# Two token-major value projections of a decoder layer as seven half-size products each, with the retention's tail among the first head products

## The chip, the core and the metric

The kernel runs on one core of a Trainium2 chip. A core has TensorE (PE; its weight loads are listed apart as PEld), VectorE (DVE), ScalarE (ACT), GpSimd (POOL) and SyncE (SP), which here only issues DMAs. The metric is the device time of one execution in microseconds (us), the median of the runs.

## The reference, cut to what matters

One layer of a hybrid decoder over 1024 prompt tokens and 8 decode tokens (one row for each of 8 samples), all float32. The part that the change touches is the mixer's input projection and what uses its value columns:

```python
hp = rmsnorm(xp, norm_mix[l])
qa, ka, va, qr, kr, vr, gr = project(hp, w_in[l])      # one product, columns split
oa = diff_attention_prompt(qa, ka, va, rel_bias, lam)  # 4 heads
s_p, o_r = retention_prompt(rotary(qr, pos_p), rotary(kr, pos_p) * kr_scale, vr.astype(f32), lg)
xp = xp + merge_groups(oa, o_r, gr, subln_a[l], lam_init).astype(xp.dtype) @ w_out[l]
...
v_prompt = jnp.stack(vp_l)                             # va is an output as well
```

`va` and `vr` are each (1024 tokens x 1024 inputs) times (1024 x 512); `gr` (the gate) and `[qr, kr]` have the same size. The retention goes through 8 chunks of 128 tokens with a state; its output is normed per head and multiplied by silu of the gate. After the mixer come memory attention and a squared-ReLU MLP.

## The kernel before, in words

**Operands.** Every large product is made from two float32r halves of each operand, a high part and what is left: high x high, high x low, low x high, three instructions that add up in one PSUM bank (`mm3`, and `mm`, line 67, through which nearly all products are issued). The inputs transposed, with the norm's gain in, lie in `UH` and `UL` (8 depth tiles of 128, 1032 columns: 1024 tokens and 8 decode rows). The norm's per-token factor `rstd1` is put on the results. Weights come in units of 128 x 1024 from `in_wall`: `unit` (line 103) issues the read on SP into a ring of three `raw` buffers, casts the high part on ACT (line 109, `wh`) and subtracts on DVE (line 110, `wl`); the rings of `wh` and `wl` have four slots.

**Order before.** (1) Query and key of the retention (`qkps`, 8 token tiles, 192 products of 512 columns) while the inputs arrive; the decode rows follow as 16 products with 40 and 8 weight columns (`decproj`, line 260). Then the token-major inputs are read again for the sums of squares (line 217), and GpSimd makes `rstd1` (line 121). (2) Retention values `vr`: 8 tiles x 24 products, with the decode rows put in between for the first two tiles (`tokproj`, `tokproj_parts`, `scaled`); the rotations of query and key run on DVE and GpSimd beside them (lines 336 to 338). (3) Three small products make the rows of the relative bias, which go through DRAM (`brow`, `brep`). (4) The retention, chunk by chunk, with the products of the gate (`grp`, 24 of 512 columns) cut into segments of 3, 4 and 1 depth tiles (`SEG`) between the small products of a chunk: transposes `tr`, scores `sc`, state `st`, output `op`. The norm and gate of a chunk (`head_norm_gate`, lines 380 to 384) run on ACT, GpSimd and DVE during the next chunk, and then `to_operand` transposes it (`trR`), splits it and stores it in DRAM (lines 393 to 396). `decode_step` does the decode rows' state. (5) Attention values `va`: 8 tiles x 24 products and decode rows; each tile is scaled on ACT and written to the output `v_p`. (6) The attention heads: `head_proj(h)` gives key and query of a head in 6 results of 24 products of 344 columns (line 67, tile `qkp`, with `UH` as the moving operand), `load_part` splits them, `fetch_values` reads `v_p` back (line 685) and `load_values` splits it (lines 695 and 697), `scores`, `turn`, `weigh` do the attention; `head_proj` of later heads is the filler between those products.

**What sets the order.** A planner orders the instructions of each engine by the order in which they are written and by when it expects operands; buffers of a tag go round, and a tile waits until the users of the slot's last tile are done. `pin[0] = True` keeps TensorE's products in the order written, and `tc.issue_after(ins)` puts the instructions of its block behind `ins` on the same engine. Each engine, and each DMA queue (SP's for most reads, ACT's, POOL's), takes its instructions in order.

## Time and profile before

| what | us |
|---|---|
| median of 3 runs | 1522.92 |
| lowest and highest run | 1519.58 and 1525.88 |
| span of the profiled execution | 1520.2 |
| TensorE busy in it | 1493.8 |
| VectorE, ScalarE, GpSimd busy | 1064.7, 653.3, 420.0 |

The span goes from the first instruction to the last; the runs' times hold some us around it. A row of the chain of waits gives start, length, engine, tile, line and the number of instructions. A row of a group gives line, engine, operation, out<-in, shapes and count, then the busy time in us and the mean of one in ns, then the idle time of the engine before these instructions and what ended it. `128*128 128x512` on a product is the weights' size and the moving operand's. Rows of the windows view give the stretch, its length, the busy time of PE, PEld, DVE, ACT and POOL with the number of instructions, the granted clock, the DMA share and GB/s. "SPq" is SP's DMA queue.

### The profile page before, as it was taken

The numbers are of one execution on the slowest core, as the hardware profiler recorded it, in microseconds if no ns is written. First come the engines' busy times: TensorE is split into PE (matmuls) and PEld (weight loads), VectorE is DVE, ScalarE is ACT, GpSimd is POOL, SyncE is SP. The second block draws the span as 40 slices with busy tenths as digits, with TensorE's granted clock in tenths as the row PEclk, the third lists the DMA queues.
The fourth block names the chain that finished last, engine by engine and source line by source line (L and its number), as shares of the span: only waits on it lengthen the run. The fifth ranks groups of instructions, "written<-read, shape, count | busy, mean of one in ns | idle before, by whom it ended". The sixth has DMA issues, their size and how long they took to land.

```text
span 1520.2 us, 26998 instructions
## 1 busy us (share of the span) xinstructions
PE 1493.8 (98%) x10587; PEld 1397.2 (92%) x10587; DVE 1064.7 (70%) x2112; ACT 653.3 (43%) x1276; POOL 420.0 (28%) x442
## 2 busy tenths in 40 slices
PE   9999999999999999999999999999999999999998
PEld 8778878999759999989999999999999999999997
DVE  4334503988865835567796978888889879787885
ACT  6423322665642432047535633333334434333454
POOL 0352212114412521124122224443335202020360
PEclk9999999999999999999999999999999999999998
DMA  8554424314755257453392334444435784636213
GB/s 299 174 147 128 103 90 110 84 51 126 232 172 218 79 206 189 128 186 104 125 338 78 117 131 148 154 140 152 142 140 164 266 281 116 191 84 195 86 43 113
DMA packets 121107, 229.25 MB, mean 151 GB/s; under 512 B 14209, under 2 KB 73712, under 8 KB 120852
## 3 DMA queue, kind: packets, MB, share of 16 engines
q1 hardware_dynamic: 89860, 172.13, 35.8%
q0 software_dynamic: 20160, 37.95, 8.2%
q10 hardware_dynamic: 10960, 17.45, 3.1%
q8 instruction: 83, 1.36, 0.4%
q14 instruction: 44, 0.36, 0.1%
HBM read 168.14 MB, written 57.52 MB: 148 GB/s over the span
## 4 chain that ended last, share of the span: by engine, by line
PE 81%; DVE 9%; DMA 4%; ACT 2%; issue 2%; POOL 0%; SPq 0%; DVEq 0%; ACTq 0%
PE dn L2000 18%; PE Z L1835 8%; PE qkp L67 7%; PE mq L67 6%; PE pr_o L67 6%; PE Y L1835 5%; PE X L1835 4%; PE pr_m L67 4%; PE vap L67 3%; PE vrp L67 3%; PE grp L67 3%; PE sp L67 2%; PE av L67 2%; PE mpv L67 1%; DVE wu L1650 1%
## 5 line engine op out<-in xcount | busy, mean ns | idle before, releaser
L2000 PE MATMUL dn<-UH,wd 128*128 128x258 f32 x1792 | 325.1, 283 | 1.6 <-ACT wd L1978 0.9
L2000 PEld LDWEIGHTS dn<-UH,wd 128*128 128x128 f32 x1792 | 277.8, 189 | 2.5 <-DVE c L2104 1.1
L2000 PE MATMUL dn<-UL,wd 128*128 128x258 f32 x896 | 253.0, 282 | 0.0
L2000 PEld LDWEIGHTS dn<-UL,wd 128*128 128x128 f32 x896 | 169.2, 189 | 0.0
L1861 ACT ACTIVATE hq<-r 128x258 f32<-128x258 f32 x128 | 53.7, 420 | 159.8 <-DVE r L1860 159.8
L2104 DVE TENSOR_TENSOR c<-c,dn 128x258 f32<-128x258 f32 x216 | 88.3, 417 | 32.5 <-PE dn L2000 31.0
L1835 PE MATMUL Z<-T_h,wu 128*128 128x258 f32 x512 | 100.0, 287 | 1.7 <-DVE u L1894 1.5
L1650 DVE TENSOR_TENSOR wu<-raw_up,wu 128x512 fp32r<-128x512 f32 x96 | 92.5, 965 | 9.5 <-ACT wu L1649 9.4
L1835 PE MATMUL X<-UH,wu 128*128 128x258 f32 x512 | 97.5, 282 | 0.0
L110 DVE TENSOR_TENSOR wl_u<-raw_u,wh_u 128x1024 fp32r<-128x1024 f32 x46 | 58.6, 1279 | 51.2 <-ACT wh_u L109 50.9
L1978 ACT CAST wd<-raw_d 128x512 fp32r<-128x512 f32 x96 | 58.5, 618 | 76.7 <-PE dn L2000 72.1
L109 ACT CAST wh_u<-raw_u 128x1024 fp32r<-128x1024 f32 x50 | 52.2, 1048 | 77.3 <-PE mq L67 42.9
L1835 PEld LDWEIGHTS Z<-T_h,wu 128*128 128x128 f32 x512 | 81.5, 189 | 4.1 <-DVE u L1894 1.9
L1971 ACT CAST UH<-raw_h 128x1032 fp32r<-128x1032 f32 x56 | 58.7, 1055 | 59.2 <-PE dn L2000 27.7
L1972 DVE TENSOR_TENSOR UL<-raw_h,UH 128x1032 fp32r<-128x1032 f32 x56 | 76.8, 1371 | 9.4 <-ACT UH L1971 9.4
L1979 DVE TENSOR_TENSOR wd<-raw_d,wd 128x512 fp32r<-128x512 f32 x96 | 75.2, 789 | 11.3 <-ACT wd L1978 11.3
L1835 PEld LDWEIGHTS X<-UH,wu 128*128 128x128 f32 x512 | 81.4, 189 | 0.2 <-ACT p L1886 0.2
L1868 POOL TENSOR_TENSOR ht<-hq 128x258 f32<-128x258 f32 x31 | 20.7, 668 | 193.2 <-ACT hq L1861 193.0
L1835 PE MATMUL Z<-T_l,wu 128*128 128x258 f32 x256 | 72.5, 283 | 0.0
L1992 POOL TENSOR_TENSOR raw_d<-raw_d,raw_d 128x512 f32<-128x512 f32 x16 | 22.0, 1378 | 182.0 <-DVE raw_d L1988 171.7
L1835 PE MATMUL X<-UL,wu 128*128 128x258 f32 x256 | 72.3, 282 | 0.0
L1649 ACT CAST wu<-raw_up 128x512 fp32r<-128x512 f32 x96 | 57.0, 610 | 27.2 <-DVE raw_up L1656 24.5
(491 smaller groups left out, 4605.6 us busy)
## 6 DMA issues: line engine op xcount, KB each, us to landing
raw_u<-in_wall SPq DMA_DIRECT2D x59, 512.0 KB, 4.5
HT<-ht POOLq DMA_DIRECT2D x32, 516.0 KB, 3.0
raw_h<-HT SPq DMA_DIRECT2D x32, 516.0 KB, 4.2
raw_up<-in_wall SPq DMA_DIRECT2D x32, 512.0 KB, 4.8
raw_d<-in_wall SPq DMA_DIRECT2D x32, 512.0 KB, 3.6
HQ<-hq ACTq DMA_DIRECT2D x32, 387.0 KB, 3.8
raw_h<-HQ SPq DMA_DIRECT2D x24, 516.0 KB, 5.2
cmk<-in_cmk SPq DMA_DIRECT2D x16, 512.0 KB, 4.7
```

The lines of the kernel that those rows point to most:

```text
L67: pinned(nc.tensor.matmul(out, l, r, start=start, stop=stop))
L110: (lo_engine or nc.vector).tensor_sub(wl[:, :n], raw[:, :n], wh[:, :n].bitcast(F32))
L1649: nc.scalar.copy(w[:, :512], src)
L1650: nc.vector.tensor_sub(w[:, 512:], src, w[:, :512].bitcast(F32))
L1835: pinned(nc.tensor.matmul(ps, l, r[:, k, :], start=first and k == 0 and x == 0, stop=k == 3 and x == 2, skip_group_check=True))
L1861: nc.scalar.activation(h[:, PLACE[quad], :], r, AF.Square)
L1971: nc.scalar.copy(h, rv)
L1972: nc.vector.tensor_sub(l, rv, h.bitcast(F32))
L1978: nc.scalar.copy(w[:, :512], src)
L1979: nc.vector.tensor_sub(w[:, 512:], src, w[:, :512].bitcast(F32))
L2000: pinned(nc.tensor.matmul(ps, l, r[:, k, cq], start=first and k == 0 and x == 0, stop=k == 3 and x == 2, skip_group_check=True))
L2104: nc.vector.tensor_add(y, y, ps)
```

## The change

The stages are put in the order 1, 5, 2, 4, 6: both value projections now stand ahead of the retention, and each is done by `token_block` as seven products q of half size (512 tokens, 512 inputs, 256 outputs; 4 token tiles x 4 depth tiles x 3 terms, two token tiles to a PSUM bank) in the order 1, 2, 6, 7, 4, 5, 3.

- **Combined inputs.** For each pair of depth tiles k and k + 4, `combine` (ACT, DVE, GpSimd) makes from the raw input rows the three combinations that the products 5, 7 and 4 need (`XT`, split in high and low), and a fourth, `t2f`, which later replaces the second half of the tokens in `UH` and `UL`, depth tiles 0 to 3, for product 6. After the products the retention's first chunks restore them from inputs that are read again (`fetch_again`, `restore`). The raw rows are kept until combined, so depth rows 3 and 7, the last to come, take the buffers of rows 0 and 4. The depth order is `KT_PAIRS` = 0, 4, 1, 5, 2, 6, 3, 7, and the weight units of query/key and of the gate are laid out to match.
- **Query and key.** Seven token tiles are done while inputs arrive, then the decode rows (`dproj`, in the eighth bank), then tile 7 alone (`last`), which takes the bank of tile 0 after `take_qk(0)`.
- **Combined weights.** `token_operands` reads the four quarters of a weight; DVE makes their sums (`s3` and others), and each product's operand is split by ACT and DVE one product ahead. The quarter 12 is read twice.
- **Results.** ACT copies product 1 and scales product 2; DVE adds the others, two banks of 512 columns each, to what is kept in SBUF. Scaling by `rstd1` is on ACT, for tiles 4 to 7 of `vr` within the retention. Decode rows go through products 1, 2, 4 and 5 with 8 instructions of 256 columns each.
- **Moved.** Rotations of tiles 8, 0, 1, 2 go into the first block and 3 to 7 into the second; the bias rows go after products 2, 6 and 7 of the first block, `brep` to chunk 3; the gate's first two units are loaded in the second block's product 5, the other two read after product 3 and split in chunk 0; ACT's silu table is loaded by a small instruction in the second block; `decode_step` is cut into pieces over chunks 0 to 3, its store goes to POOL's queue, as does the read of `rb`; the decode outputs (`opd`) go to chunk 5.
- **The tail.** The first head's units are loaded in chunk 7. After the retention come 36 products of the first head, then `to_operand` of chunk 7, then the rest.

The diff, cut to its core:

```diff
+    def behind(*engines):
+
+        st = ExitStack()
+        for e in engines:
+            last = next(x for x in reversed(nc.cur_bb.bb.instructions) if str(x.engine).split(".")[-1] == e)
+            st.enter_context(tc.issue_after(last))
+        return st
...
+    def combine(k, y1, y2):
+
+        g1, g2 = g_mix[:, k : k + 1], g_mix[:, k + 4 : k + 5]
+        t2 = t2f[k // 2][:, k % 2, :]
+        nc.scalar.activation(y1[:, f_lo], y1[:, f_lo], AF.Copy, scale=g1)
+        nc.scalar.activation(dd[:, k, :], y1[:, NT:], AF.Copy, scale=g1)
+        nc.scalar.activation(y2[:, f_lo], y2[:, f_lo], AF.Copy, scale=g2)
+        nc.vector.scalar_tensor_tensor(y1[:, f_hi], y1[:, f_hi], g1, y1[:, f_lo], ALU.mult, ALU.subtract)
+        nc.vector.scalar_tensor_tensor(t2, y2[:, f_hi], g2, y1[:, f_hi], ALU.mult, ALU.subtract)
+        nc.vector.scalar_tensor_tensor(dd[:, k, :], y2[:, NT:], g2, dd[:, k, :], ALU.mult, ALU.subtract)
+        nc.gpsimd.tensor_sub(y1[:, f_lo], t2, y1[:, f_lo])
+        nc.gpsimd.tensor_sub(y2[:, f_lo], y2[:, f_lo], t2)
+        for q, src in ((5, y1[:, f_hi]), (7, y1[:, f_lo]), (4, y2[:, f_lo])):
+            h, l = (x[:, k, :] for x in XT[q])
+            nc.scalar.copy(h, src)
+            nc.vector.tensor_sub(l, src, h.bitcast(F32))
...
+            if kt > 5:
+                combine(kt - 6, rows.pop(kt - 6), rows.pop(kt - 2))
...
+        dproj(qkps[7], units_qk)
...
+        with behind("Activation", "DVE", "Pool"):
+            combine(2, rows.pop(2), rows.pop(6))
+            combine(3, rows.pop(3), rows.pop(7))
...
+            def operand(q):
+                if q == 1:
+                    load(11)
+                    load(12, True)
+                    load(22)
+                    load(21)
+                    return split(raws[11], q)
+                if q == 2:
+                    return split(raws[12], q)
+                if q == 6:
+                    a22, a21, a11 = raws[22], raws[21], raws[11]
+                    s3 = raws[7] = G.tile([P, 1024], F32R, tag="wl", name=f"s3_{nm}", bufs=RING).bitcast(F32)
+                    nc.vector.tensor_sub(s3, a11, a21)
+                    nc.vector.tensor_sub(a11, a22, s3)
+                    return split(a11, q)
+                if q == 4:
+                    w = split(raws[22], q)
+                    nc.vector.tensor_add(raws[21], raws[21], raws[22])
+                    return w
+                if q == 5:
+                    w = split(raws[21], q)
+                    load(12)
+                    return w
+                if q == 3:
+                    nc.vector.tensor_sub(raws[12], raws[12], raws[11])
+                    return split(raws[12], q)
+                return split(raws[7], q)
...
+        take_qk(0, qkps[0], 1)
+        take_qk(1, qkps[1], 0)
+        last = PS0.tile([P, 512], F32, tag="acc", name="qkp_7l", bufs=8)
+        for kt in KT_PAIRS:
+            wh, wl = units_qk[kt % 4]
+            ws, tk = slice((kt // 4) * 512, (kt // 4) * 512 + 512), slice(7 * P, 8 * P)
+            mm(last, UH[:, kt, tk], wh[:, ws], kt == 0, False)
+            mm(last, UH[:, kt, tk], wl[:, ws], False, False)
+            mm(last, UL[:, kt, tk], wh[:, ws], False, kt == 7)
+        op_va(1)
...
+            RIGHT = {1: (UH, UL, 0, 0), 2: (UH, UL, 4, 0), 6: (UH, UL, 0, 512), 3: (UH, UL, 4, 512)}
+            RIGHT.update({q: (*XT[q], 0, 0) for q in XT})
...
+            order = (1, 2, 6, 7, 4, 5, 3)
+            for n, q in enumerate(order):
+                w = ready(q)
+                if q in (1, 6):
+                    more()
+                    more()
+                if n < 6:
+                    ready(order[n + 1])
+                if n == 5:
+                    after()
+                if q in fetch:
+                    with behind("SP"):
+                        fetch_rot(fetch[q])
+                xh, xl, k0, c0 = RIGHT[q]
+                kind = "x" if q in (1, 2) else "y" if q in (5, 3) else "z"
+                for pb in range(2):
+                    if q in (1, 6, 5):
+                        banks[kind, pb] = PS.tile([P, 512], F32, tag=kind, name=f"{nm}p_{kind}_{pb}", bufs=2)
+                    ps = banks[kind, pb]
+                    for j in range(2):
+                        tk = slice(c0 + (2 * pb + j) * P, c0 + (2 * pb + j) * P + P)
+                        for k in range(4):
+                            wk = [y[:, k * 256 : k * 256 + 256] for y in w]
+                            for x, (l, r) in enumerate(((xh, wk[0]), (xh, wk[1]), (xl, wk[0]))):
+                                pinned(nc.tensor.matmul(
+                                    ps[:, j * 256 : j * 256 + 256], l[:, k0 + k, tk], r,
+                                    start=q in (1, 6, 5) and (j, k, x) == (0, 0, 0), stop=(k, x) == (3, 2), skip_group_check=True))
+                    pv = ps.rearrange("p (j c) -> p j c", j=2)
+                    lo, hi = acc[pb], acc[-2 + pb]
+                    a, b = slice(0, 256), slice(256, 512)
+                    with behind("Activation", "DVE"):
+                        if q == 1:
+                            nc.scalar.copy(lo[:, :, b], pv)
+                        elif q == 2:
+                            for j in range(2):
+                                nc.scalar.activation(lo[:, j, a], pv[:, j, :], AF.Copy, scale=rstd1[:, 2 * pb + j : 2 * pb + j + 1])
+                        else:
+                            into, plus = {6: (hi[:, :, a], lo[:, :, b]), 7: (hi[:, :, b], lo[:, :, b]), 4: (lo[:, :, b],) * 2,
+                                          5: (hi[:, :, b],) * 2, 3: (hi[:, :, a],) * 2}[q]
+                            nc.vector.tensor_add(into, pv, plus)
+                        if q in (4, 3):
+                            for j in range(2):
+                                scale((0 if q == 4 else 4) + 2 * pb + j)
+                if q in (1, 2, 4, 5):
+                    d0, cd = {1: (0, 0), 2: (4, 0), 4: (8, 256), 5: (0, 256)}[q]
+                    for k in range(4):
+                        for x, n in ((0, 40), (1, 8)):
+                            pinned(nc.tensor.matmul(
+                                psd[:n, cd : cd + 256], UD[:, d0 + k, :n], w[x][:, k * 256 : k * 256 + 256],
+                                start=(q, k, x) == (1, 0, 0), stop=(k, x) == (3, 1), skip_group_check=True))
+                    if q == 5:
+                        merge_parts(psd, out_dec, nm)
+                        nc.scalar.activation(out_dec, out_dec, AF.Copy, scale=rstd1[:8, 8:9])
+                with behind("Activation", "DVE", "SP"):
+                    between(q, acc)
...
+        def after_va(q, acc):
+            if q == 1:
+                for k in range(4):
+                    src = t2f[k // 2][:, k % 2, :]
+                    nc.scalar.copy(UH[:, k, f_hi], src)
+                    nc.vector.tensor_sub(UL[:, k, f_hi], src, UH[:, k, f_hi].bitcast(F32))
+            if q in (2, 6, 7):
+                next(bias)
+            for t in {4: range(4), 3: range(4, 8)}.get(q, ()):
+                nc.scalar.dma_start(o["v_p"][t * P : t * P + P, :], acc[t // 2][:, t % 2, :])
+            if q == 5:
+                nc.scalar.dma_start(o["v_s"], vdec)
+            if q in rot_va:
+                rotate(rot_va[q])
...
+            if t < 4:
+                with behind("DVE", "Pool", "Activation"):
+                    nc.scalar.activation(vr[t + 4], vr[t + 4], AF.Copy, scale=rstd1[:, t + 4 : t + 5])
+                    if t % 2:
+                        next(dec)
+                    else:
+                        restore(t // 2, 0)
+                        restore(t // 2, 1)
...
+        fill(36)
+        to_operand(gate, P, 7, "7", ("ah", "al", 2))
```

More of the change, by code (lines that the diff above doesn't have):

```diff
@@ L170, in decoder_step @@
             nc.tensor.matmul(qkps[7][:, :P], idle, idle, start=True, stop=True)
-        units_qk = []
-        for kt in range(8):
+        units_qk, rows = [], {}
+        for kt in KT_PAIRS:
+            rx = rows[kt] = front_row(A, kt)
             if kt == 0:
@@ new lines, in rotate @@
+        def rotate(t):
+            n = P if t < 8 else 8
+            q, rot = qk[t], rots[t]
+            qv = q[:n].rearrange("p (a b c) -> p a b c", b=2, c=32)
+            sv = rot[:n, 512:1024].rearrange("p (a b c) -> p a b c", b=2, c=32)
+            with behind("DVE"):
+                for b in range(2):
+                    nc.vector.tensor_mul(sv[:, :, b, :], qv[:, :, 1 - b, :], sv[:, :, b, :])
+            nc.gpsimd.tensor_mul(q[:n], q[:n], rot[:n, 0:512])
+            nc.gpsimd.tensor_add(q[:n], q[:n], rot[:n, 512:1024])
@@ L358, in decoder_step @@
-        pin[0] = False
-        for g in (dec, *first):
-            next(g, None)
-        for t in range(8):
-            scaled(t, ps2[t] if t < 2 else tokproj(units, t, f"vrp_{t}", PS)[0], P)
-            if t == 4:
-                with tc.issue_after(nc.cur_bb.bb.instructions[-1]):
-                    scaled(8, vr[8], 8)
-        nc.sync.dma_start(vrd, vr[8][:8])
+        maskM = A.tile([P, 512], F32, tag="maskM", name="maskM")
+        nc.sync.dma_start(maskM, i["maskM"])
+        for x in range(2):
+            with behind("SP"):
+                fetch_again(x)
@@ L468, in decoder_step @@
             nc.vector.tensor_mul(Sm, sc, maskM)
+            if t == 0:
+                with behind("Activation", "DVE"):
+                    units += [unit(U_TOK + 10 + u, raw=late_raws[u]) for u in range(2)]
             st = PS.tile([P, 512], F32, tag="st", name=f"st_{t}", bufs=1)
```

351 lines of the change are left out of this document (205 added, 146 removed).

## The prediction

> **What bounds the kernel now.** I read the page's head first, then the chain of work that ended last, then the groups of instructions by form, then the timelines of the first 60 us. The head and the chain's shares:
>
> ```profile
> span 1520.2 us, 26998 instructions
> PE 1493.8 (98%) x10587; PEld 1397.2 (92%) x10587; DVE 1064.7 (70%) x2112; ACT 653.3 (43%) x1276; POOL 420.0 (28%) x442
> PE 81%; DVE 9%; DMA 4%; ACT 2%; issue 2%; POOL 0%; SPq 0%; DVEq 0%; ACTq 0%
> ```
>
> TensorE is busy 98% of the span and carries 81% of the chain; VectorE 9%. So almost only what shortens TensorE's stream shortens the kernel. The stretch of the change is the first 242 us, in the chain in order of time (start, length, what, count):
>
> ```profile
> 5.74 45.34 PE qkp L67 x192
> 51.08 3.69 PE qkp L260 x16
> 55.70 2.79 PE vrp L67 x12
> 63.14 2.81 PE vrp L67 x12
> 66.89 36.14 PE vrp L67 x156
> ...
> 188.64 0.70 PE grp L67 x3
> 189.34 3.72 PE vap L260 x16
> 193.06 5.57 PE vap L67 x24
> 199.07 16.70 PE vap L67 x72
> 219.30 11.32 PE vap L67 x48
> 230.96 11.36 PE vap L67 x48
> ```
>
> From 5.74 to 242.32 the chain is a nearly unbroken run of products: query/key (qkp), retention values (vrp), the retention with its gate (grp), attention values (vap). The stretch is bound by the product stream, 232 ns apiece at 512 columns (36.14/156). Idle time of TensorE up to 290 us, by who ended it:
>
> ```profile
> PE trA L70 <- DVE e L737: 1.2, 1, 1.2
> PE qkp L170 <- DVE ss L211: 1.1, 1, 1.1
> PE qkp L67 <- DVE qraw L645: 1.0, 1, 1.0
> ```
>
> 3.3 us in all, so a gain there has to come from fewer or shorter products.
>
> **The products.** vrp's main products are three runs of 12 (the first and the last are quoted, 2.79 and 2.81; the middle one is 2.81 too) and one of 156: 2.79+2.81+2.81+36.14 = 44.55 us for 192, vap's 5.57+16.70+11.32+11.36 = 44.95 us: 89.50 us together. Each projection becomes seven products of half size in tokens, depth and width: 4 token tiles x 4 depth tiles x 3 terms = 48 instructions of 256 columns, 336 per projection, 672 in all. No value product of 256 columns runs before, but the same kind does later, in memory keys and values; the last row is the MLP's 258 columns:
>
> ```profile
> 645.89 5.70 PE mk L67 x48
> 739.83 1.70 PE mpv L67 x12
> 873.66 2.87 PE X L1835 x24
> L67 PEld LDWEIGHTS mpv<-mph,wh_kv x64: 185/188/194, 692.6 to 753.8; 128*128 128x128 f32 x64
> ```
>
> That is 118.8, 141.7 and 119.6 ns apiece. The 141.7 is the only one with waits around it; I take 118.8, the longest pure run, and keep 141.7 as the bad end. 672 x 118.8 = 79.8 us, so 9.7 us leave. The decode rows were 16 products of 512 columns per projection, 3.72 us, 7.4 for two; they become 4 x 8 of 256 columns, 64 x 118.8 = 7.6 us, +0.2. Net **-9.5 us**. Query/key keeps 192 + 16 products (tile 7 is only done last), the retention keeps its own, the bias row products and the one for decode outputs move: 0.
>
> The weight load takes 188 ns (last row), over the pitch of 118.8, so loads already run under one another. The Trainium skill, "TensorE: Matmul & The Clock Gate", section "Back-to-back issue gap", says that spacing in a stream of loads and products is set by both together and gives about 81 ns at 128 columns and 131 ns at 512, so that halving the columns saves less than half. Halfway (an estimate from that page, 106 ns) two half products would cost 212 against 131 and the change would lose; here 118.8 against 232 is a clean half, and the rows decide for the sum; rival 5 keeps the other way.
>
> **What must hide behind the products.** A seven-product scheme adds sums of operands, sums of results, and a combined form of the inputs. Prices, ns of one, VectorE, then ACT and GpSimd:
>
> ```profile
> L110 DVE TENSOR_TENSOR wl_u<-raw_u,wh_u 128x1024 fp32r<-128x1024 f32 x17 | 20.7, 1222 | 36.6 <-ACT wh_u L109 36.5
> L336 DVE TENSOR_TENSOR t<-qk,rot 128x256 f32<-128x256 f32 x16 | 12.8, 838 | 14.9 <-DMA rot<-in_rot 13.5 <-POOL qk L337 1.4
> L394 DVE TENSOR_TENSOR rl<-trR,rh 128x512 fp32r<-128x512 f32 x8 | 5.5, 688 | 5.0 <-ACT rh L393 4.9
> L109 ACT CAST wh_u<-raw_u 128x1024 fp32r<-128x1024 f32 x17 | 17.8, 1047 | 11.1 <-DMA raw_u<-in_wall 4.4 <-PE vrp L67 3.5 <-PE vap L67 2.4
> L393 ACT CAST rh<-trR 128x512 fp32r<-128x512 f32 x8 | 4.7, 586 | 19.8 <-PE trR L70 19.8
> L337 POOL TENSOR_TENSOR qk<-qk,rot 128x512 f32<-128x512 f32 x8 | 10.3, 1291 | 4.2 <-DVE t L336 4.2
> ```
>
> DVE in the block of attention values, each at its nearest row: 7 splits (six of its own, the next block's first) 8.5; four operand sums of 1024 at 1.22, 4.9; ten result sums of 512 at 0.69, 6.9; four low halves rewritten, 2.8; rotation of three tiles (two ops of 0.84 each) and the short one, 5.9; one merge 0.7. Sum 29.7 us. TensorE has there 39.9 of products, 3.8 of decode rows and 2.2 of bias rows: 45.9. In the retention values' block: 8 splits (two are the gate's units) 9.8, sums 4.9, results 6.9, five rotations 8.4, merge 0.7: 30.7 against 43.7 us. The cover is there as a whole (65% and 70%); what counts is order, as DVE takes these in the order written. The engines were mostly idle there before:
>
> ```profile
> 60.00:80.00 20.00, 20.00 (x88) 15.49 (x87) 8.04 (x13) 5.43 (x8) 15.21 (x11) 1.00 0.60 203
> 200.00:220.00 20.00, 20.00 (x79) 13.71 (x79) 0.56 (x1) 3.21 (x5) 1.54 (x2) 1.00 0.29 79
> ```
>
> DVE 8.0 and 0.6 of 20 us, ACT 5.4 and 3.2. ACT gets 7.3 of casts (7 x 1.05), 2.5 of input copies and some 10 of results, scalings and bias rows per block, 20 of 45.9, besides the issue of the stores of `v_p`, which go from SP's queue to ACT's; in the second also the table load of the gate's function, which merely moves. The DMAs added are one quarter of each weight read twice and two reads of inputs, 2.1 MB in 90 us, on engines busy 0.60 and 0.29 in these rows. I walked through both blocks product by product (5.7 us, 6.6 with decode rows), DVE in program order:
> - Attention values, third product (q=6): ahead of its operand DVE has to rewrite four low halves, which wait for ACT's copies that sit behind product 1's result (6.3 us into the block); they end at 9.5, the two operand sums at 11.9, ACT's cast at 13.0, the low part at 14.3. TensorE wants it at 13.2. **+1.2**.
> - Last product (q=3): its bank waits for product 5's sum, behind operand 3, the next block's first split: **+0.4**.
> - Retention values: the banks of q=4 come free 0.2 us early, others 1 us or more: **+0.3**. Its last product's results and the gate's first units then run into the retention: gate units 10 and 11 are split only after the first mask product, 0.2 late, and DVE and ACT have restoring of UH/UL and scaling of four tiles in the first four chunks: **+0.3**.
>
> Bounds of these four waits: 0 (another order of writing) to 6 (each one a whole result sum and split later).
>
> **The front.** Query/key runs seven tiles per depth row, so rows are wanted after 21 products (4.9 us) instead of 24 (5.6). The second row's low part:
>
> ```profile
> 9.98 1.29 DVE L126 SCALAR_TENSOR_TENSOR UL<-x,g_mix,UH 128x1032 fp32r<-128x1032 f32 x1 [1.44 <-ACT UH L125]
> 17.70 13.48 SPq L215 DMA_DIRECT2D xt<-in_xtok  x9
> 36.66 1.83 POOL L121 TENSOR_TENSOR rstd<-ss,half 128x9 f32<-128x9 f32 x1 [36.22 <-DVE ss L120]
> ```
>
> It ends at 11.27. Products start at 5.6, the first ones slow by 0.9 us, so it is wanted at 11.4: no wait, by 0.1. Rows 3 and 7 now wait on SP for the buffers of rows 0 and 4, which the first combination frees (ACT 1.6, DVE 1.4, GpSimd 1.3 each for two sums, three casts and three subtractions; after the sixth row, some 18 us, done by 24). They are wanted at 35 and 40: hidden. Behind them in SP's queue stand the token rows (17.70 before, now about 24.5), so the row factors, written by GpSimd at 38.5, come at 45 to 48. The second weight quarter waits on SP for a slot that tile 7's first products free, at 50.6, with two quarters behind it:
>
> ```profile
> raw_u<-in_wall SPq DMA_DIRECT2D x59, 512.0 KB, 4.5
> ```
>
> At 4.5 us apiece and half overlapped all are there by 57; the first is wanted for a split at 60: hidden. New: tile 7's products need the bank of tile 0, so its scaling, so the row factors. They begin at 45.5 + 3.7 = 49.2. Cost 0, margin 1 to 3 us; queued behind that wait is everything of TensorE.
>
> **The end of the stretch.** The last chunk's norm and gate now stand behind the last retention chunk, and the first head products are put ahead of its transposes, 36 of them. The second head product's bank is one that the last chunk's output holds. That chain, in the chunk before:
>
> ```profile
> 178.47 0.28 ACT L380 ACTIVATE jk<-op 128x128 f32<-128x128 f32 x1 [4.08 <-PE op L67]
> 182.14 1.13 DVE L384 SCALAR_TENSOR_TENSOR gate<-op,r,gate 128x128 f32<-128x128 f32 x4 [0.57 <-POOL r L121]
> ```
>
> Squares begin 0.1 after the output product, the gate is done at 183.27, 4.9 us after it. TensorE has 0.70 of gate products, 0.34 of small transposes and 24 head products (3.8): 4.8. **+0.1**; without the head products ahead it would be 4. The head's first units are split as slots of the gate's come free within chunk 7. Removed: the values of head 0 are stored some 100 us sooner, so their read, ACT's and GpSimd's casts and the loads queued on SP behind them no longer meet the head's start:
>
> ```profile
> 245.39 6.21 DMA vraw<-out_v_p
> 256.97 4.50 DMA hm<-in_hm
> 261.50 0.20 DVE dmn L939
> ```
>
> The query scaling that held TensorE 1.0 us stood in DVE's queue behind the load ending at 261.47. That load was issued behind the second read on SP, itself held by GpSimd: **-1.0**. The 1.2 us at the first transposes is the softmax's own start and stays.
>
> **Sum.** -9.5 + 1.2 + 0.4 + 0.3 + 0.3 + 0.1 - 1.0 = **-8.2 us**. The profiled execution's span is 1520.2 and the median 1522.92 of 1519.58 to 1525.88; the 2.7 us between are taken as unchanged, so 1522.9 - 8.2 = **1514.7 us**. Own range 1511 (waits 0, and half of the 1.2 too) to 1519 (waits of 6 instead of 2.3).
>
> **Rivals.**
> 1. *No waits at all*: results always come in time, and the softmax's start is covered too: -9.5 - 1.0 - 1.2 = -11.7, **1511**. For it: DVE's load of 65 to 70%. Against: the order above.
> 2. *The front comes late*: the row factors wait for token rows behind the held rows 3 and 7, and DVE does two more combinations (3.8 us each) ahead of tile 0's scaling. TensorE stands at 49.2 for about 5 us: **1519.7**. For: the margin is 1 to 3 us on a queue of nine loads. Against: factors are ready before and the loads had waits of their own.
> 3. *DVE becomes the bound of both blocks*, on the other side. The point is 43.7/30.7 = 1.42 times the prices above. Rows that show such a growth, two pairs of the same rotation:
>
> ```profile
> 69.85 1.16 DVE L336 TENSOR_TENSOR t<-qk,rot 128x256 f32<-128x256 f32 x2 [4.60 <-DMA rot<-in_rot]
> 79.56 2.61 DVE L336 TENSOR_TENSOR t<-qk,rot 128x256 f32<-128x256 f32 x2 [1.84 <-DMA rot<-in_rot]
> ```
>
> 2.25 times, with GpSimd busy through the second. Rotations (2.6 us of GpSimd each) now run beside the splits and operand sums. At 1.83, halfway from 1.42 to 2.25, the blocks take 54.4 and 56.2 us instead of 45.9 and 43.7: +21.0, so -9.5 + 21.0 + 2.3 - 1.0 = +12.8, **1535.7**. Against: GpSimd is used 21 us in 90 there, and result sums read PSUM. The Trainium skill, "SBUF — State Buffer", section "SBUF: two separate sides", says that a VectorE instruction with two SBUF inputs and a GpSimd one that reads SBUF exclude each other for a whole instruction. The 1.16 and 2.61 agree with such a wait of one GpSimd instruction; it bears on this rival's price, for the splits and operand sums.
> 4. *It does not do what it says*: the half products go at 141.7 ns. 736 x 141.7 = 104.3 against 96.9 now: +7.4, with 2.3 of waits and the 1.0 removed +8.7, **1531.6**. Against: 48 in 5.70 without a wait.
> 5. *Weight loads bound the pitch*, 188 ns: 736 x 188 = 138.4, +41.5, with the rest (+0.2 is in it) 1522.9 + 41.5 + 2.3 - 1.0 = **1565.7**. Against: every pitch row. The Trainium skill's page and section named above lead there: its 106 to 131, put on our 232, gives 188 as well.
>
> **Chances.** Forecast 0.52, rival 1 0.14, rival 2 0.12, rival 3 0.14, rival 4 0.05, rival 5 0.01, something not seen 0.02 (slower). 0.5% is 7.6 us, about what a measurement of this kernel can tell from no change: faster ends at 1515.3, slower begins at 1530.5. The forecast's 0.52 lies 0.31 below 1515.3 and 0.21 above, so faster 0.31 + 0.14 = 0.45, same 0.21 + 0.12 = 0.33, slower 0.22. The range takes the forecast, rivals 1 and 2 and the near edge of rival 3 and leaves 0.2 out: **1509 to 1530**.
>
> **What would show it.** In the profile after: 24 half products of one bank at 2.85 us; the second block's last value product ending near 146 (54.8 + 45.9 + 1.6 + 43.7 + 0.3); TensorE idle in the first block about 1.6 us, released by DVE's low part of the third operand; none before 54.8; DVE 65 to 70% busy from 55 to 146; the wait of the head's query scaling gone. The prediction is wrong if TensorE idles over 3 us at 49 (rival 2), if DVE's 1024-element split is over 1.7 us in the blocks (rival 3), or if the half product's pitch is over 125 ns (rival 4).

## The result, and the profile after

| what | us |
|---|---|
| kernel before, median of 15 runs | 1520.62 (1516.63 to 1525.88) |
| changed kernel, median of 15 runs | 1527.39 (1520.99 to 1533.34) |
| ratio, with 95% interval | 1.0036 [1.0021, 1.005] |
| profiled execution of the changed kernel, its span | 1523.67, 1521.6 |

The change makes the kernel slower by 0.36%, where 0.54% faster was forecast. Among the executions of the kernel before that stand beside runs 5 to 8 below, one took 1715.78 us at a mean clock of 0.79 and is left out. The ratios here and below stand as recorded with their intervals; they are not plain quotients of the medians (1.0045 here). The head of the page of the changed kernel, its engines and the chain's shares:

```profile
span 1521.6 us, 27763 instructions
PE 1484.8 (98%) x10907; PEld 1407.6 (93%) x10907; DVE 1124.1 (74%) x2188; ACT 673.5 (44%) x1320; POOL 436.9 (29%) x449
PE 73%; DVE 12%; DMA 6%; issue 3%; ACT 3%; POOL 1%; SPq 0%; ACTq 0%; DVEq 0%; POOLq 0%
```

TensorE is busy 9.0 us less (1493.8 before), so work did leave. It came back as waiting: its share of the chain falls from 81 to 73%. TensorE's waits up to 300 us in the changed kernel (total, times, longest), to be read beside the three rows of before:

```profile
PE qkp_7l L75 <- ACT qk L399: 5.3, 1, 5.3
PE qkp L75 <- DVE kraw L878: 2.1, 2, 1.4
PE trA L78 <- DVE e L975: 1.2, 1, 1.2
...
PE vap_y L486 <- DVE va L501: 0.5, 1, 0.5
PE vrp_x L486 <- DVE wl_vr L118: 0.2, 1, 0.2
PE vrp_z L486 <- DVE wl_vr L118: 0.2, 1, 0.2
```

The first row is new, and it is the largest single wait: tile 7's products wait until a scaling by the row factors has read a bank and freed it. What leads there is the chain of the changed kernel, in order of time:

```profile
30.76 4.18 ACT xt L277 x8
34.96 5.12 DMA xt<-in_xtok
40.16 2.19 ACT xt L277 x4
...
44.69 2.28 POOL x L189
46.97 1.71 POOL x L190
49.35 1.55 DVE TF4l L194
50.91 1.15 DVE dd L188
...
54.14 0.02 ACT le L299
...
54.25 0.68 ACT qk L399
...
54.97 8.53 PE qkp_7l L75 x24
63.50 5.68 PE vap_x L486 x48
```

The squares of the token rows end at 42.35; then come the rows of two combinations on ScalarE, VectorE and GpSimd (L183 to L194). TensorE is released by ScalarE's first scaling (L399), which stands behind a small exponential (L299) that waits for VectorE's rows behind the combinations. VectorE's scaling of tile 0 (L397) starts at 54.64 and takes 0.74, so it ends after TensorE has gone on at 54.97: the bank that tile 7 got is not tile 0's, as the section on the change has it, but one that ScalarE frees. The scalings of both engines stand behind the same combinations and start within 0.4 us of each other, so the argument stays; "tile 0's scaling" below is VectorE's.

The 24 products take 8.53 us, and 24 x 232 ns are 5.57. The windows show why; the column behind POOL's is the granted clock:

```profile
54.00:56.00 2.00, 1.03 (x3) 0.84 (x4) 1.76 (x8) 1.86 (x4) 0.00 (x0) 0.52 0.00 0
56.00:58.00 2.00, 2.00 (x6) 1.61 (x5) 1.95 (x5) 0.68 (x3) 0.00 (x0) 0.50 0.00 0
...
60.00:62.00 2.00, 2.00 (x9) 1.59 (x8) 1.23 (x1) 0.00 (x0) 0.00 (x0) 0.77 0.31 25
62.00:64.00 2.00, 2.00 (x13) 1.75 (x12) 0.46 (x1) 0.00 (x0) 0.00 (x0) 1.00 0.41 33
63.50:109.00 45.50, 44.98 (x363) 41.81 (x362) 24.62 (x29) 16.34 (x26) 6.89 (x4) 1.00 0.40 138
109.00:155.24 46.24, 45.87 (x384) 44.80 (x383) 30.00 (x37) 17.79 (x26) 27.10 (x17) 1.00 0.51 167
```

After the wait TensorE has half its clock until about 61 us. A busy digit of 2.00 of 2.00 hides that; only the clock column and the count of products (6 in a window of 2 us, where windows at clock 1.00 before the wait hold 10 or 11) show it.

**The ledger of the two profiled executions, up to the attention.** Front: the first value product starts at 63.50 instead of 54.8, +8.7 (5.3 of waiting, 3.0 of clock, 0.4 net of smaller things, among them a wait of 0.6 for the second depth row's low part, where the prediction expected none). Value blocks: 63.50 to 155.24 is 91.74, less 2.2 of bias rows 89.5, where the products and decode rows took 96.9 before: -7.4. The head's start: the wait of 1.0 became 2.1, +1.1. That makes +2.4; the first transposes of the attention (`trA`) start at 276.9 instead of 274.0, +2.9, so 0.5 isn't assigned. Behind that the two executions come nearly level again: the MLP's first product (`X`) starts at 848.1 and 847.8, and at 850.8 in a second profile of the kernel before (run 11). The spans differ by 1.4 only, the medians by 6.8: single executions vary more than that, 1516.6 to 1525.9 for the kernel before. These two profiles show where the change costs, not the whole 6.8. Mean clock and span go together: over the 15 runs of the changed kernel a straight line gives 1.3 us for each 0.001 of clock, and the profiled one had 0.996 where the median is 0.994. So the profile shown was one of its faster runs.

### The profile page after: what moved, and what is told of

Its sections match the earlier page's. It is cut to its first block, busy times and chain, and to the rows that moved or that the text cites. A ratio compares the mean times of both kernels' runs of the same rounds, so it can differ in the third digit from the quotient of the medians.

```text
span 1521.6 us, 27763 instructions
## 1 busy us (share of the span) xinstructions
PE 1484.8 (98%) x10907; PEld 1407.6 (93%) x10907; DVE 1124.1 (74%) x2188; ACT 673.5 (44%) x1320; POOL 436.9 (29%) x449
## 4 chain that ended last, share of the span: by engine, by line
PE 73%; DVE 12%; DMA 6%; issue 3%; ACT 3%; POOL 1%; SPq 0%; ACTq 0%; DVEq 0%; POOLq 0%
PE dn L2239 17%; PE Z L2074 7%; PE pr_o L75 6%; PE mq L75 5%; PE Y L2074 5%; PE X L2074 4%; PE pr_m L75 4%; PE qkp L75 4%; PE grp L75 3%; PE sp L75 2%; PE av L75 2%; DVE wu L1889 1%; PE mpv L75 1%; PE vap_z L486 1%; DMA raw_up<-in_wall 1%
## 5 line engine op out<-in xcount | busy, mean ns | idle before, releaser
L117 ACT CAST wh_u<-raw_u 128x1024 fp32r<-128x1024 f32 x43 | 44.5, 1047 | 68.5 <-PE mq L75 42.9
L118 DVE TENSOR_TENSOR wl_u<-raw_u,wh_u 128x1024 fp32r<-128x1024 f32 x39 | 49.5, 1275 | 21.2 <-ACT wh_u L117 21.1
```

The costliest lines, as they stand in the source:

```text
L118: (lo_engine or nc.vector).tensor_sub(wl[:, :n], raw[:, :n], wh[:, :n].bitcast(F32))
```

## The experiments

What was open: why tile 0 is scaled so late; what the fall of the clock costs; whether the head's wait is the table load. The texts on record speak of theories by letter or number; in short, the first four runs set the order of the queues (row factors, or tile 0's scaling, behind the combinations) against the time that the combinations themselves take. Runs 1 to 4, 5 to 8, 9 and 10, 11 and 12 each share their runs of the kernel before; across these groups only ratios are compared. The intervals of runs 1, 2, 4, 5, 6 and 9 overlap the changed kernel's own, [1.0021, 1.005], so what these edits are worth is read from their profiles, one execution each; those of runs 3, 7 and 10 lie below it.

**1. Tile 0's scaling first.** The scaling is issued ahead of the last two combinations.

```diff
+        with behind("Activation", "DVE", "Pool"):
+            nc.vector.tensor_scalar(qk0, qkps[0], rstd1[:, 0:1], None, ALU.mult)
         with behind("Activation", "DVE", "Pool"):
             combine(2, rows.pop(2), rows.pop(6))
```

> The scaling of tile 0 by its row factors is put ahead of the last two combinations of inputs on VectorE; nothing else changes. Theory A (TensorE waited 5.3 us because that scaling stood in the queues of VectorE and ScalarE behind those combinations, and the granted clock fell because of that idle time, so that the 24 products after it took 8.5 instead of 5.6 us): no wait there, 24 products in 5.6 us, 8.3 us less than the changed kernel, ratio to the kernel before 0.997 to 0.999. Rival B (the slow 24 products have another cause than the idle time): they stay at 8.5 us and only 5.3 us come back, ratio 1.000 to 1.002. Rival C (the combinations are then late for the value products): a new wait of 2 us or more in the first value block, ratio 1.001 or above.

Measured: 1526.84 us, ratio 1.0047 [1.0031, 1.0063]. Its waits:

```profile
PE vap_x L488 <- ACT wh_va L117: 7.4, 1, 7.4
PE vap_x L488 <- DVE wl_va L118: 0.7, 1, 0.7
```

Tile 7's wait is gone, and 8.1 us stand one step on, at the first value products: their operand's cast and split stand behind the combinations and the other tiles' scalings. This is what rival C expected. The first value product is at 62.09, against 63.50, but the next one, which needs the low part, only at 63.35, so nearly nothing is gained. So the scaling's place alone is not the cause; the combinations hold the queues for whatever comes next.

**2. The wait filled.** 23 products without use, ahead of the decode rows (5.3 us), so that TensorE does not stand.

```diff
+        for n in range(23):
+            mm(qkps[7], UH[:, 0, 0:P], units_qk[3][0][:, 0:512], True, True)
         dproj(qkps[7], units_qk)
```

> The changed kernel with 23 idle products of 512 columns (5.3 us, their result is overwritten) ahead of the query/key decode rows, so that TensorE is busy while the scaling of tile 0 is late. Theory A: the end of the wait stays at about 55 us, but the granted clock stays at 1.0 and tile 7's 24 products take 5.6 us, so 3 us come back: ratio to before 1.001 to 1.002. Rival B: the 24 products stay at 8.5 us and nothing comes back, ratio 1.0035 or above.

Measured: 1523.3 us, ratio 1.002 [1.0004, 1.0036]. The window of this kernel in which the changed one had half its clock:

```profile
55.00:60.00 5.00, 4.80 (x21) 3.90 (x22) 3.32 (x6) 3.44 (x6) 0.00 (x0) 1.00 0.00 0
```

The clock stays at 1.00, and the first value product starts at 61.41, 2.1 earlier than in the changed kernel, although nothing else was helped. That is theory A. Idle time thus cost more than itself: work that does nothing is cheaper here than waiting.

**3. The combinations' subtractions on VectorE.** Two lines of `combine`:

```diff
-        nc.gpsimd.tensor_sub(y1[:, f_lo], t2, y1[:, f_lo])
-        nc.gpsimd.tensor_sub(y2[:, f_lo], y2[:, f_lo], t2)
+        nc.vector.tensor_sub(y1[:, f_lo], t2, y1[:, f_lo])
+        nc.vector.tensor_sub(y2[:, f_lo], y2[:, f_lo], t2)
```

> The two subtractions of each combination go from GpSimd to VectorE. If the late scaling comes from VectorE instructions stretched by GpSimd beside them (1.6 to 1.8 us instead of 0.68), the last combination ends 2 to 4 us earlier than 53.9 us and the wait shrinks from 5.3 to 2 or 3 us, ratio 1.000 to 1.002. If it comes from the sheer amount of work ahead of the scaling in VectorE's queue (4 more subtractions of 0.69 us), the wait stays near 5 us, ratio 1.003 or above.

Measured: 1517.61 us, ratio 0.9989 [0.9974, 1.0003]. The chain of this kernel:

```profile
45.25 3.70 PE qkp L209 x16
48.95 5.58 PE qkp_7l L75 x24
54.53 5.68 PE vap_x L486 x48
```

No wait, full clock, first value product at 54.53, earlier than before the change. One edit takes all 9.0 us out of the front. This is more than either text on record had given (2 us of wait or more left, 1.000 or above). Taken alone it speaks for GpSimd beside VectorE as the cause; run 5 corrects that.

**4. Run 1 with the tables early.** Seven small reads for the decode rows (`idx`, `pt`, `idk`, `pos`, `sel`, `hm`, `relb`) are issued with the first head's units instead of behind them.

```diff
+            nc.sync.dma_start(idk, bcast_rows(i["page_table"], P, 16))
+            nc.sync.dma_start(pos, i["pos"])
+            nc.sync.dma_start(sel, i["sel"])
+            nc.sync.dma_start(hm, i["hm"])
...
         head_units(1)
+        tables()
```

> factors_first, and the seven small tables of the paged decode attention are read at the start of the head stage, ahead of the units and values on SyncE's queue. Theory: the head's key and query scalings stood on VectorE behind instructions that wait for these tables (until 261.0 us), so 2.1 us of waits at the head's start go and the kernel is 1 to 2 us faster than factors_first, ratio to before 0.996 to 0.998. Rival: the chain of splits and of GpSimd's copies behind them ends as late anyway, and the 2.1 us show up at the first scores or transposes: same as factors_first.

Measured: 1525.38 us, ratio 1.0045 [1.003, 1.0061]; run 1's 1.0047 lies inside, as the rival has it. The wait of the head's products falls from 3.2 to 1.3 and the 1.2 at `trA` goes, but the time does not show it.

**5. Only the last two combinations on VectorE**, to see whether those between 43 and 54 us decide.

```diff
+        e = nc.vector if k > 1 else nc.gpsimd
+        e.tensor_sub(y1[:, f_lo], t2, y1[:, f_lo])
+        e.tensor_sub(y2[:, f_lo], y2[:, f_lo], t2)
```

> The changed kernel with the two subtractions of the last two combinations (those after the token rows) on VectorE and those of the first two left on GpSimd. Theory 1 (GpSimd beside VectorE between 44 and 52 us is what makes the front late): no wait of TensorE at 49 to 55, first value product at 54.5 to 55, granted clock 1.0 from 40 to 60, 1517 to 1519 us, ratio 0.998 to 1.000. Rival (the chain is late because all four combinations lie behind each other, and the first two count as much): a wait of 1 to 3 us stays ahead of tile 7, first value product at 56 to 60, 1520 to 1524 us.

Measured: 1528.96 us, ratio 1.0035 [1.002, 1.0051]: theory 1 falls, and the rival's 1 to 3 us is too little as well. The first value product comes at 60.95, 2.5 earlier than in the changed kernel, and the time doesn't show it. VectorE in this kernel, then its wait:

```profile
43.42 0.75 DVE L186 SCALAR_TENSOR_TENSOR x<-x,g_mix 128x512 f32<-128x512 f32 x1 [0.44 <-ACT x L183]
...
47.36 0.69 DVE L195 TENSOR_TENSOR TF7l<-x,TF7h 128x512 fp32r<-128x512 f32 x1
...
53.25 2.73 DVE L398 TENSOR_SCALAR qk<-qkp,rstd 128x512 f32<-128x512 f32 x4
```

```profile
PE qkp_7l L75 <- ACT qk L400: 4.7, 1, 4.7
```

Nothing is stretched (0.69), and still TensorE waits 4.7 us. The chain begins at 43.42; in run 3 it begins at 38.05. The difference is in SP's queue, in the changed kernel:

```profile
16.84 3.27 SPq L250 DMA_DIRECT2D x<-in_xT  x2
...
21.68 14.03 SPq L276 DMA_DIRECT2D xt<-in_xtok  x9
```

and in run 3:

```profile
12.76 0.81 SPq L276 DMA_DIRECT2D xt<-in_xtok  x2
21.30 0.93 SPq L250 DMA_DIRECT2D x<-in_xT  x2
22.28 9.15 SPq L276 DMA_DIRECT2D xt<-in_xtok  x7
```

With all subtractions on VectorE the planner put two token rows ahead of depth rows 3 and 7; in the other kernels so far all nine stand behind them. So run 3's edit of two lines changed the order of the reads as well. The row factors start at 37.69 in run 3, at 42.63 in the changed kernel, and the last two combinations are written behind them.

**6. GpSimd work that nobody reads**, in run 3's kernel, behind the third combination:

```diff
             combine(2, y1, y2)
+            for n in range(3):
+                nc.gpsimd.tensor_sub(y1[:, f_lo], y1[:, f_hi], y1[:, f_lo])
```

> The kernel with all subtractions on VectorE, and three GpSimd subtractions of the same size added behind the third combination, on a dead row: nobody reads their result. Theory 1 (GpSimd and VectorE hold each other up): VectorE's operations between 44 and 49 us, 0.68 to 0.75 us without them, show 1.2 us or more, three GpSimd ones 1.5 to 2.3 us, tile 0's scaling comes 1 to 4 us later than 47.88 and TensorE waits 0.5 to 3.5 us ahead of tile 7; first value product at 55 to 60. Rival (it was only that GpSimd's link in the chain is slow and comes in turn with VectorE's): VectorE's operations keep 0.68, tile 0 is scaled at 47.9, no wait, time as without them, 1517.6.

Measured: 1524.61 us, ratio 1.0003 [0.9984, 1.0022]. GpSimd of this kernel, then VectorE beside it:

```profile
43.08 5.15 POOL L283 TENSOR_TENSOR x<-x 128x512 f32<-128x512 f32 x3 [3.24 <-DVE TF7l L194]
```

```profile
43.52 1.78 DVE L187 SCALAR_TENSOR_TENSOR t2f<-x,g_mix,x 128x512 f32<-128x512 f32 x1
45.23 1.26 DVE L188 SCALAR_TENSOR_TENSOR dd<-x,g_mix,dd 128x8 f32<-128x8 f32 x1
...
47.01 1.77 DVE L190 TENSOR_TENSOR x<-x,t2f 128x512 f32<-128x512 f32 x1
48.71 0.68 DVE L194 TENSOR_TENSOR TF5l<-x,TF5h 128x512 fp32r<-128x512 f32 x1
...
51.38 2.73 DVE L400 TENSOR_SCALAR qk<-qkp,rstd 128x512 f32<-128x512 f32 x4
```

Three VectorE instructions take 1.0 us more each (0.74 to 1.78, 0.22 to 1.26, 0.68 to 1.77), the three GpSimd ones 1.72 each against 1.29 alone, and tile 0 is scaled at 51.38 instead of 47.88 (ScalarE's first scaling at 50.98 instead of 47.48). The wait is 2.9 us, the first value product at 57.70. The stretching is real, 3.5 us on this chain for three subtractions that nobody needs; it is the second half of the cause. In the changed kernel it is worth less, since without GpSimd VectorE has four subtractions more to do; run 9 gives the size. The Trainium skill, "SBUF — State Buffer", section "SBUF: two separate sides", says that a VectorE instruction with two SBUF inputs and a GpSimd one that reads SBUF lock one another out for a whole instruction. These rows agree.

**7. Run 3 with the tables early.**

> The kernel with all subtractions on VectorE and the seven small tables of the decode rows read at the start of the attention heads instead of behind the first heads' units. Theory 1 (the tables, queued on SP behind unit reads that wait for a buffer, hold the softmax's constants and behind them the head's query scaling): the wait of the head's products falls from 2.2 to under 1.3 us, the one of 1.2 at the first transposes goes, 1515.5 to 1517 us, ratio 0.9975 to 0.9985. Rival (those waits are taken up by the next one): same time as without the move, 1517.6, ratio 0.999.

Measured: 1518.23 us where before took 1522.14 (34 runs), ratio **0.9969 [0.9951, 0.9988]**: this version is faster than both kernels. Its waits between 230 and 300 us:

```profile
PE sp L75 <- DMA KB<-KB: 0.5, 1, 0.5
PE qkp L75 <- DVE kraw L878: 0.2, 1, 0.2
```

Run 3's 2.2 at the head's products is 0.2 here, its 1.2 at `trA` is gone. That this made the step from 0.9989 to 0.9969 isn't shown, since the intervals overlap.

**8. The kernel before with the tables early.**

> The kernel before with the same move of the seven small tables. By the step of the prediction (the wait of 1.0 us of the head's products is the tables' load) that wait goes and with it up to 1.2 at the first transposes: 1518.3 to 1519.6 where the kernel before takes 1520.6, ratio 0.9985 to 0.9993. Rival (something else is ready as late): same time, ratio 1.000.

Measured: 1522.2 us, ratio 0.9992 [0.9975, 1.0009]. The profile has no wait of TensorE left between 230 and 300 us, `trA` starts at 271.9 instead of 274.0: the table load did hold the head's start. Its size isn't fixed: the unchanged kernel, profiled again (run 11), shows 1.7 at the head's products, and moved in time (run 12) none. Whether the whole kernel gains the 1 us can't be told.

**9. Two token rows first**, all subtractions left on GpSimd.

```diff
+            if kt == 3:
+                for t in (1, 3):
+                    raw = A.tile([P, D], F32, tag="xt", name=f"xt_{t}", bufs=2)
+                    nc.sync.dma_start(raw, i["xtok"][t * P : t * P + P, :])
+                    nc.scalar.activation(raw, raw, AF.Square, accum_out=ss[:, t : t + 1])
             rx = rows[kt] = front_row(A, kt)
```

> The changed kernel, all its GpSimd subtractions kept, with two of the nine token rows (read and squared for the row factors) written ahead of depth rows 3 and 7 instead of behind them. Theory 2 (the front is late for two reasons of about the same size: the token rows are read behind the two held depth rows, so that the row factors come at 42.6 instead of 37.7 us, and GpSimd beside VectorE stretches what then lies ahead of tile 0's scaling): row factors start at 37 to 39 us, the chain of combinations stays 11 to 12 us long, tile 0 is scaled at 49 to 51, TensorE waits 0 to 2 us, its clock stays at 1.0, first value product at 54.5 to 57, 1518 to 1521 us, ratio 0.999 to 1.000. Theory 1 (GpSimd beside VectorE alone): the wait stays at 3 to 5 us, 1522 to 1526. Rival (rows 3 and 7 now come late instead, since the token rows take their place in the queue): the query/key products wait 1 to 4 us before 45.

Measured: 1523.57 us, ratio 1.0021 [1.0009, 1.0034]. The chain of this kernel, then its windows:

```profile
45.80 1.70 DVE TF4l L194
47.50 1.17 DVE dd L188
...
51.59 7.40 PE qkp_7l L75 x24
58.99 5.68 PE vap_x L491 x48
```

```profile
52.00:54.00 2.00, 2.00 (x7) 1.62 (x6) 2.00 (x5) 1.27 (x3) 0.00 (x0) 0.60 0.00 0
54.00:56.00 2.00, 2.00 (x6) 1.52 (x6) 0.62 (x2) 1.41 (x2) 0.00 (x0) 0.55 0.08 23
```

The factors start at 39.23 and the wait is 2.4 instead of 5.3, so theory 1 alone falls again; but theory 2 had put it at 2 at most and the time at 1521 at most. Two things were missed: the factors come 1.5 us later than in run 3, and the clock did fall (1.8 of the delay). The rival's sign is there too, under its size: the query/key products wait 0.9 us for a depth row. The four kernels together (factors start; wait ahead of tile 7; first value product):

| | subtractions on GpSimd | the last two or all on VectorE |
|---|---|---|
| token rows behind depth rows | 42.63; 5.3; 63.50 | 43.06; 4.7; 60.95 (run 5) |
| two token rows ahead | 39.23; 2.4; 58.99 | 37.69; 0; 54.53 (run 3) |

The order of the reads is worth 4.5 and 6.4 us at the first value product, the subtractions 2.5 and 4.5, and both together 9.0. (Runs 3 and 5 also differ in the first two combinations.) The profiles separate the two on one chain, from VectorE's first row of the last two combinations to ScalarE's first scaling. With GpSimd it takes 11.25 and 11.28 us (43.00 to 54.25 in the changed kernel, 39.59 to 50.87 here), without it 9.42 and 9.43 (43.42 to 52.84 in run 5, 38.05 to 47.48 in run 3). So GpSimd's part lengthens the chain by 1.8, and the order of the reads moves its start by 3.4 to 5.4. Of the 9.0 between the changed kernel and run 3, 6.0 are the later release (5.0 by the start and 1.8 by the length, less 0.8 that run 3 has in hand) and 3.0 the slow clock.

**10. The same with the tables early.**

> The same with the seven small tables of the decode rows read at the start of the attention heads. Theory 2: as the run above, and the waits of the first head's products (3.2 us in the changed kernel's kind) fall under 0.5 us: 1515.5 to 1518.5 us, ratio 0.997 to 0.999. Rival (the head's waits are taken up again later, as they were in the kernel before, where the same move left the time within its interval): as the run above, 0.999 to 1.000.

Measured: 1520.79 us, ratio 0.9997 [0.998, 1.0014]. The head's waits fall from 2.1 and 1.2 to 1.3 and 0; the ratio lies in the rival's range and just outside theory 2's, and the interval takes in both.

**11 and 12. A wait 800 us later.** All ten profiles with the change show the MLP's second stream of products (`Z`) waiting 0.5 to 3.3 us for a sum that stands behind the split of a late weight; the kernel before and run 8 show no such wait, with the same order of instructions there. The kernel before was profiled again, unchanged, and with 23 products without use ahead of its first.

> The kernel before, unchanged, for a further profile of it. In all ten profiles of kernels with the change, the MLP's second matrix product stream waits 0.5 to 3.3 us (2.2 on average) for a sum of results behind a weight read that lands late; in the two profiles of kernels without the change this wait does not appear, although the instructions stand in the same order there. Theory (it belongs to the change, by when its reads fall): 0 again. Rival (it is chance of the run): 0.5 to 3.3 us here too.

> The kernel before with 23 idle products of 512 columns ahead of its first real ones, which moves TensorE's stream by 23 x 0.232 = 5.3 us at most. Same question, with the whole kernel moved in time as the late front moves it: theory (the wait belongs to the change's own later reads or places in memory, not to the moment): 0 again; rival (chance, or the moment): 0.5 to 3.3 us.

Measured: 1524.28 and 1526.54 us, one run each, beside 1526.06 for the kernel before. Unchanged, it has none again; moved in time, it has this row:

```profile
PE Z L1837 <- DVE u L1891: 2.1, 1, 2.1
```

So a kernel without the change can get this wait too, when its start is moved. In the changed kernel the weight read that it hangs on takes 5.3 us from issue to use (1033.64 to 1038.96) against 3.7 before (1032.37 to 1036.03). Which transfers it meets there was not found; one shifted profile suggests the moment, and doesn't prove it.

## Why the prediction was wrong, step by step

- **Products, -9.5: right in kind, 1.2 too much.** Half products go at 118 to 125 ns (48 in 5.68 to 5.99 us), 118.8 was taken. With decode rows and waits the blocks take 89.5; without the 0.9 of waits 88.6, where the products took 96.9, so -8.3. Neither the 141.7 ns of rival 4 nor rival 5's weight loads came.
- **Waits in the blocks, +1.2, +0.4, +0.3: 1.0 too high together.** The 1.2 for the third operand didn't come; the 0.4 for a bank behind product 5's sum was 0.5, and in the second block low parts of operands were late by 0.2 and 0.2. Forecast were 96.9 - 9.5 + 1.9 = 89.3 for both blocks, and 89.5 came: two errors cancel there, which is luck. VectorE is busy 24.62 of 45.5 and 30.00 of 46.24 us, 54 and 65%; rival 3 did not come, though three of the 14 splits took 1.95 to 2.33 us, over the 1.7 that the prediction had named as its sign.
- **The front, "Cost 0, margin 1 to 3 us": this step failed.** The row factors were forecast for 45 to 48 and were there at 44.46, earlier. What failed is the sentence that set them against 49.2 as if the scaling followed at once. In the queues of VectorE and ScalarE two combinations stand between, and their first step on ScalarE stands behind the same squares. That is rival 2, given 0.12: "about 5 us" there, 5.3 measured. The agreement is partly luck: two combinations of 3.8 us behind the factors were counted, while the chain took 11.25 and began at 43.00, ahead of them. Its price lacked two things: GpSimd and VectorE stretching one another on that chain (run 6), and the half clock behind the wait (run 2). The front cost 8.7, not 5.
- **The head's wait, -1.0: failed too.** The read of `v_p` did hold the table load in the kernel before, and it is gone from there; but another hold took its place. In the chain of the changed kernel a unit's split frees the buffer for the next unit's read, and the tables are queued on SP behind that read:

```profile
250.87 1.24 DVE wl_u L118
253.93 1.02 SPq L1099
255.00 6.02 DMA hm<-in_hm
```

  It was issued 2.0 earlier than before (255.00 against 256.97) but took 6.02 from issue to landing instead of 4.50. So it landed at 261.02 (261.47 before), and the wait grew from 1.0 to 2.1. Runs 7 and 8, which move the load itself, leave 0.2 and 0 of it, runs 4 and 10 leave 1.3, so the load is not the whole of it.
- **The 0.3 in the retention and the 0.1 at its end:** no wait of TensorE shows there in this profile.
- **The sum.** By the profiles -7.4 + 8.7 + 1.1 = +2.4 up to the attention, and +2.9 with what isn't assigned, instead of -8.2. 1527.39 lies inside 1509 to 1530, but on the wrong side of no change, in the part that was there for rival 3, which didn't come. The rest of the 6.8 between the medians isn't assigned; the later `Z` wait (2.2 on average in ten profiles) and the mean clock, which varies from run to run, are in it. Nor is the late front all that the forecast lacked: in run 3, which has none, `trA` starts at 267.8, 6.2 earlier than before the change, and still the time falls by 0.11% (at most 0.26% by the interval), not by 0.54%. Its `Z` wait is 3.3; what else is lost behind the attention's start wasn't found.

## What to carry to other kernels

When a bank or a buffer that the busiest engine needs is released by another engine, ask not when that engine's operands are ready but what is queued ahead of the release, and price each of these instructions beside its neighbours. Count the wait of TensorE with the slower clock behind it. A saving of 7 us in the products is worth what the chain ahead of them leaves of it; here an edit of two lines, which moved subtractions to the engine that seemed the fuller one and changed the order of the reads with it, gave the front back.

## What the runs showed of the hardware

- After a wait of 5.3 us TensorE's granted clock was 0.50 for about 6 us (24 products in 8.53 instead of 5.57); after 4.7 (run 5) 0.50 and 0.65 in two windows of 2 us, 7.38 for the 24; after 2.4 us (run 9) 0.60 and 0.55, 7.40; after 1.9 us (run 10) 0.60 and 0.55, 7.38; after 2.9 us (run 6) it stayed at 1.00. So the length of the wait alone doesn't set the price. The Trainium skill, "TensorE: Matmul & The Clock Gate", section "What's actually happening", gives half clock after an idle window of about 3.4 us that runs freely, and full clock after a busy one. The halving agrees; the 2.4 and 1.9 us that sufficed in runs 9 and 10 are shorter than that window, and the measurement decides.
- In run 6 one GpSimd subtraction of 512 columns cost the VectorE instruction beside it 1.0 us, whether that was one of 512 columns (0.74 to 1.78) or of 8 (0.22 to 1.26).
